# Tokens regrouped by residue modulo 16, and one transposition moved from TensorE to VectorE

## The chip, the cores and the metric

The kernel runs on one core of a Trainium2 chip. A core has five engines that run side by side, each with its own instruction queue that is worked off strictly in order: TensorE (PE in the profile; its weight loads are shown apart as PEld), VectorE (DVE), ScalarE (ACT), GpSimd (POOL) and SyncE (SP). They wait for one another through semaphores. Sixteen DMA engines move data between the core's memory SBUF and HBM; the transfers are issued from the queues of SP, ACT and POOL. Matrix products land in PSUM. The metric is the time of one execution on the device, in microseconds.

## The reference

Two layers over 512 tokens of width 1024. Layer 0 is attention in three groups of 8 heads; in each group a token sees keys at a stride (the dilation) within a window, and the three results are mixed by their log-sum-exp:

```
A_GROUPS = ((128, 1), (512, 4), (2048, 16))      # (window, dilation)
for g, (window, dilation) in enumerate(A_GROUPS):
    # query t attends to t + j*dilation, |j| <= window/(2*dilation)
    o_g, l_g = dilated_window_attention(q[:, :, g], k[:, :, g], v[:, :, g], window, dilation)
w = softmax(stack(lses), axis=2);  o = sum(w[..., None] * outs)
```

With 512 tokens the third group (dilation 16) lets a token see exactly the 32 tokens of its own residue modulo 16. Layer 1 is grouped-query attention over all tokens with a rotary embedding by row and column. Both layers also attend to 256 memory tokens, multiply by a SiLU gate, go through an output projection and are added to the residual: `x = x + y @ w_out`.

## The kernel before

**Tokens.** The 512 tokens stand in four blocks of 128, one token a partition. Block `c` (or `b`) holds the tokens whose residue modulo 4 is `c`: partition `p` holds token `4p + c`. The views that say so are `xv` (L1053, the input, read again at L1003 for the residual sum), `v0w` (L1182, a scratch tensor `v0d` in HBM that takes the values of the first group) and `ov` (L1671, the output); the rotary tables are laid out likewise on the host. So the second group (dilation 4) needs scores within a block only, and so does the third: its scores are the same 128x128 products with a mask that keeps keys of the same residue modulo 4 within the block, which is modulo 16 over all tokens. The first group (dilation 1) needs the tokens in their natural order; `qk0` is written in that order with a stride (L1264, L1265), and its values go through `v0d`.

**Projections.** Each projection is a seven-product scheme (`s_chunk`, L390) with matmuls at L176, L177 and L180. Weights come as 512 KB tiles `wl` on SP's queue (L261), some are summed by POOL's accumulating DMAs (L297, L307) or by DVE (L292), ACT makes a rounded copy `wh` (L323) and DVE the rest `wo` (L333). A ring of four such pairs feeds TensorE.

**The order of the work.** One core, no scheduler: a driver (`Driver`, L48) counts slots, one for each group of projection matmuls, and in between lets generators place the attention work of the head before. The text of every engine's queue follows from the slots alone.

**The start.** Memory tokens first, while `x` is loaded in four transfers (L1071); ACT squares `x` (L527), POOL makes the factor, DVE scales (L534), TensorE transposes (L540). `setup` (L1097) loads the mask and the rotary tables.

**A head of layer 0.** `head_chunk` (L1230) projects, `attn_a` (L1274) attends. Scores `sa` come from L1301 (first group, `o = 0`) and L1305 (second and third, `o = 1`); DVE adds the mask and takes the maximum (L1311), ACT makes exponentials (L1283), statistics go through HBM (`ds`) to change between the two token orders, `scale` (L1372) weights the probabilities, and `turn` (L1381) transposes them on TensorE into PSUM `pt` (L1392) and copies them to SBUF `pT` (L1396 for `o = 1`, `split` for `o = 0`). For `o = 1` there are two parts of four 128x128 blocks: `k = 0` is the second group, copied by ACT, `k = 1` the third, copied by DVE. `pv` (L1407) multiplies by the values, `comb` (L1421) adds the two orders.

**The end.** The last output projection stores eight pieces of 256 KB: four on ACT's queue as they are ready (L1674), the last four on ACT's and SP's (L1682).

Of the kernel before, what the change touches and what calls it, by code (L numbers as in the profile page):

```python
# [131 lines left out]
def trunk_kernel(ctx: ExitStack, tc: tile.TileContext, x, mem, wall, norm_g, mem_norm_g, gcol,  # L132
# [857 lines left out]
    def out_proj(YW, ys, src, evac, tiles, half=False, last=None):  # L990
# [10 lines left out]
        def ev(q, u, t):  # L1001
            b, n = 2 * (int(q[0]) - 1) + u, int(q[1]) - 1
            G.dma_start(t, src[b][:, n * 512:(n + 1) * 512], accum_op=ALU.add)  # L1003
            yield 2
            done.add((n, b))
# [47 lines left out]
    xv = x.rearrange("(p c) d -> c p d", c=4)  # L1053
# [43 lines left out]
    def setup():  # L1097

        nc.sync.dma_start(mask, mask_d)
        nc.sync.dma_start(tabA, tab_a.rearrange("p (b c d) -> p b c d", b=2, c=4))  # L1100
        nc.sync.dma_start(grA[:, 0:3], qn_a[0:1, :, 0:32].to_broadcast([128, 3, 32]))
        nc.sync.dma_start(grA[:, 3:6], kn_a[0:1, :, 0:32].to_broadcast([128, 3, 32]))
        yield 4
        V.tensor_tensor(gk, gc[:, 0:3], gc[:, 3:6], ALU.mult)
        V.tensor_scalar(gk, gk, QS, None, ALU.mult)
        V.tensor_scalar(gc[:, 6:8], gc[:, 6:8], QS, None, ALU.mult)
        V.memset(gk[0:32, :], 1.0)
        V.tensor_scalar(grA[:, 0:3], grA[:, 0:3], QS, None, ALU.mult)
# [121 lines left out]
    def head_chunk(h):  # L1230
# [7 lines left out]
        def ev(q, u, t):  # L1238
# [19 lines left out]
            def put():  # L1258
# [3 lines left out]
                else:  # L1262
                    A.copy(qs[:, :, cs], p[:, 1:3])
                    A.copy(qk0[:, 0].rearrange("p (a c) -> p c a", c=4)[:, b], p[:, 0])  # L1264
                    V.tensor_scalar(qk0[:, 1].rearrange("p (a c) -> p c a", c=4)[:, b], p[:, 3], gk[:, 0:1], None, ALU.mult)  # L1265
# [8 lines left out]
    def attn_a(h, qk0, qs, ks, v12, n_done):  # L1274
# [64 lines left out]
        nc.sync.dma_start(nat_v[:, :, 0, :], stp[:, 0])  # L1339
        nc.sync.dma_start(str_v[:, :, 1, :], stp[:, 1])  # L1340
        yield Y[3]
        nc.sync.dma_start(oth[:, 0], nat_v[:, :, 1, :])
        nc.sync.dma_start(oth[:, 1], str_v[:, :, 0, :])
# [37 lines left out]
        def turn(o):  # L1381

            if o:
                parts = [[(b, k) for b in range(4)] for k in range(2)]
                pts[o] = m4(name="pT").rearrange("p (k t) -> p k t", k=2)
            else:
                parts = [[(0, 0), (3, 1), (0, 1), (1, 0)], [(1, 1), (2, 0), (2, 1), (3, 0)]]
                pts[o] = [m4(F32R, "pT") for _ in range(2)]
            for i, part in enumerate(parts):
# [4 lines left out]
                def copy(pt=pt, i=i):  # L1394
                    if o:
                        (V.tensor_copy if i else A.copy)(pts[o][:, i], pt)  # L1396
# [10 lines left out]
        def pv(o):  # L1407
# [13 lines left out]
            def comb():  # L1421
                if o:
                    A.copy(rs, oo)
                else:
                    V.tensor_tensor(rs.rearrange("p (b a) -> p b a", b=4), oo.rearrange("p (a b) -> p b a", b=4),
                                    rs.rearrange("p (b a) -> p b a", b=4), ALU.add)
# [51 lines left out]
    def setup_b():  # L1478
        tb_raw = s2(name="tbraw").rearrange("p (c b e) -> p c b e", c=2, b=4)
        nc.sync.dma_start(tb_raw, tab_b.rearrange("p (c b e) -> p c b e", c=2, b=4))  # L1480
# [190 lines left out]
    ov = out.rearrange("(p c) d -> c p d", c=4)  # L1671

    def ev_o2(n, b, o):
        nc.scalar.dma_start(ov[b][:, n * 512:(n + 1) * 512], o[n])  # L1674
# [6 lines left out]
    def last_o2(n, b, t, c):  # L1681
        (nc.sync if n else nc.scalar).dma_start(ov[b][:, n * 512 + c.start:n * 512 + c.stop], t[:, c])  # L1682
# [107 lines left out]
```

## Time and profile before

| what | value |
|---|---|
| three runs, median (lowest to highest) | 943.32 us (943.01 to 944.55) |
| the profiled execution, first to last instruction | 940.4 us |
| PE, PEld busy | 932.0 us (99%), 819.4 us (87%) |
| DVE, ACT, POOL busy | 799.6, 691.6, 348.4 us (85%, 74%, 37%) |
| TensorE clock granted | 1.000 |
| DMA traffic | 207.15 MB in 89285 packets |

The page gives no other time for the profiled execution than its span; the median of the runs is 2.9 us above that. Durations in the profile are of single instructions, which overlap on an engine that pipelines them, so a busy time is a union and not a sum. The DMA share is the mean over the sixteen DMA engines, and it can pass 1.

### The profile page before, as it was taken

The numbers are of one execution on the slowest core, as the hardware profiler recorded it, in microseconds if no ns is written. First come the engines' busy times: TensorE is split into PE (matmuls) and PEld (weight loads), VectorE is DVE, ScalarE is ACT, GpSimd is POOL, SyncE is SP. The second block draws the span as 40 slices with busy tenths as digits, with TensorE's granted clock in tenths as the row PEclk, the third lists the DMA queues.
The fourth block names the chain that finished last, engine by engine and source line by source line (L and its number), as shares of the span: only waits on it lengthen the run. The fifth ranks groups of instructions, "written<-read, shape, count | busy, mean of one in ns | idle before, by whom it ended". The sixth has DMA issues, their size and how long they took to land.

```text
span 940.4 us, 16301 instructions
## 1 busy us (share of the span) xinstructions
PE 932.0 (99%) x5500; PEld 819.4 (87%) x5500; DVE 799.6 (85%) x1443; ACT 691.6 (74%) x1720; POOL 348.4 (37%) x494
## 2 busy tenths in 40 slices
PE   8999999999999999999999999999999999999998
PEld 6889888888888888888889998888988999999886
DVE  6998776879888888889788999877998998689978
ACT  7775788677768686867675768537878887789773
POOL 3412425455554545463836111214252440110122
PEclk9999999999999999999999999999999999999999
DMA  9999937869787878696867979979985686785777
GB/s 346 387 259 324 316 93 189 278 133 262 155 251 146 261 155 267 158 268 136 242 177 190 269 202 249 291 239 317 270 201 118 171 240 167 198 225 121 200 159 179
DMA packets 89285, 207.15 MB, mean 220 GB/s; under 512 B 25201, under 2 KB 34417, under 8 KB 89202
## 3 DMA queue, kind: packets, MB, share of 16 engines
q1 hardware_dynamic: 68674, 140.51, 43.5%
q0 software_dynamic: 19520, 63.97, 36.8%
q10 hardware_dynamic: 1008, 1.64, 0.5%
q8 instruction: 43, 0.70, 0.3%
q14 instruction: 40, 0.33, 0.1%
HBM read 158.31 MB, written 11.08 MB: 180 GB/s over the span
## 4 chain that ended last, share of the span: by engine, by line
PE 95%; DVE 2%; ACT 1%; DMA 1%; issue 0%; SPq 0%; DVEq 0%; ACTq 0%
PE pj L177 25%; PE pj L176 25%; PE pj L180 25%; PE qT L645 3%; PE sa L1305 2%; PE oo L1413 2%; PE pt L1392 1%; PE ptb L1619 1%; PE sa L1301 1%; PE xT L540 1%; PE ob L180 1%; PE ob L177 1%; PE ob L176 1%; PE sb L171 1%; PE sb L170 1%; PE sb L172 1%
## 5 line engine op out<-in xcount | busy, mean ns | idle before, releaser
L333 DVE TENSOR_TENSOR wo<-wl,wh 128x1024 fp32r<-128x1024 f32 x258 | 316.3, 1232 | 6.9 <-ACT wh L323 6.7
L323 ACT CAST wh<-wl 128x1024 fp32r<-128x1024 f32 x258 | 272.1, 1061 | 31.0 <-PE pj L177 17.4
L176 PE MATMUL pj<-wh,hS 128*128 128x512 f32 (+1 forms) x416 | 154.4, 380 | 0.0
L177 PE MATMUL pj<-wh,hS 128*128 128x512 f32 (+1 forms) x416 | 149.0, 367 | 0.0
L176 PE MATMUL pj<-wh,h 128*128 128x512 f32 (+1 forms) x312 | 115.3, 378 | 0.0
L177 PE MATMUL pj<-wh,h 128*128 128x512 f32 (+1 forms) x312 | 111.7, 367 | 0.0
L488 POOL TENSOR_TENSOR rstd<-mse,half 128x4 f32<-128x4 f32 (+2 forms) x98 | 103.4, 1056 | 8.2
L180 PE MATMUL pj<-wo,hS 128*128 128x512 f32 (+1 forms) x416 | 99.5, 366 | 0.0
L177 PEld LDWEIGHTS pj<-wh,hS 128*128 128x128 f32 x416 | 78.7, 189 | 11.2
L176 PEld LDWEIGHTS pj<-wh,hS 128*128 128x128 f32 x416 | 78.6, 189 | 11.1 <-DVE sn L420 0.2
L487 POOL TENSOR_SCALAR mse<-hss 128x4 f32<-128x4 f32 (+1 forms) x88 | 47.8, 543 | 101.9 <-ACT junk L633 94.2
L180 PEld LDWEIGHTS pj<-wo,hS 128*128 128x128 f32 x416 | 72.5, 189 | 13.1
L633 ACT ACTIVATE junk<-sn 128x128 f32<-128x128 f32 x264 | 79.4, 311 | 2.7 <-DVE sn L411 2.6
L398 ACT COPY sn<-pj 128x512 f32<-128x512 f32 x122 | 67.1, 588 | 17.8 <-PE pj L180 17.0
L1249 POOL TENSOR_TENSOR ta<-sn,tabs 128x128 f32<-128x128 f32 (+1 forms) x64 | 35.8, 566 | 119.0 <-DVE sn L638 91.8
L180 PE MATMUL pj<-wo,h 128*128 128x512 f32 (+1 forms) x312 | 74.5, 365 | 0.0
L307 POOL DMA_DIRECT2D wl<-wl x34 | 30.2, 897 | 113.3 <-DVE wo L333 73.3
L261 POOL DMA_DIRECT2D wl<-in_wall_dram x40 | 38.0, 966 | 80.4 <-DMA wl<-in_wall_dram 41.0
L177 PEld LDWEIGHTS pj<-wh,h 128*128 128x128 f32 x312 | 59.0, 189 | 8.4
L176 PEld LDWEIGHTS pj<-wh,h 128*128 128x128 f32 x312 | 59.0, 189 | 8.2
L420 DVE TENSOR_TENSOR sn<-pj,sn 128x512 f32<-128x512 f32 x89 | 60.8, 684 | 5.7 <-PE pj L180 5.3
L180 PEld LDWEIGHTS pj<-wo,h 128*128 128x128 f32 x312 | 54.3, 189 | 9.7
(290 smaller groups left out, 2367.2 us busy)
## 6 DMA issues: line engine op xcount, KB each, us to landing
wl<-in_wall_dram SPq DMA_DIRECT2D x224, 512.0 KB, 7.4
wl<-wl POOLq DMA_DIRECT2D x68, 512.0 KB, 5.5
wl<-in_wall_dram POOLq DMA_DIRECT2D x44, 512.0 KB, 8.5
od<-o SPq DMA_DIRECT2D x11, 256.0 KB, 5.4
og<-od SPq DMA_DIRECT2D x10, 256.0 KB, 9.5
x<-in_x_dram SPq DMA_DIRECT2D x4, 512.0 KB, 9.1
v0d<-sn SPq DMA_DIRECT2D x8, 256.0 KB, 8.5
acc<-in_x_dram POOLq DMA_DIRECT2D x8, 256.0 KB, 6.2
```

What stands on the lines that cost most here:

```text
L176: T.matmul(o, a, b, start=start, stop=False, skip_group_check=True)
L177: T.matmul(o, c, d, start=False, stop=False, skip_group_check=True)
L180: T.matmul(o, a, b, start=False, stop=stop, skip_group_check=True)
L261: queue.dma_start(t, wall[d], **how)
L323: A.copy(wh, self.tile[self.items[i]])
L333: V.tensor_tensor(wo, self.tile[key], wh.bitcast(F32), ALU.subtract)
L398: A.copy(t, b)
L420: V.tensor_tensor(t, b, t, ALU.subtract if q == "12" else ALU.add)
L487: G.tensor_scalar(e, ss, EPS, None, ALU.add)
L488: G.tensor_tensor(r, e, half[:, 0:n], ALU.pow)
L633: A.activation(jk, p[:, j * 128:(j + 1) * 128], AF.Square, scale=by, accum_out=ss[:, j:j + 1])
L1249: G.tensor_tensor(ta[:, 0:n], xn[:, 0:n, 0:32], ropeA[:, 0, b, s0:s0 + n], ALU.mult)
```

## The change

Within a block the tokens now stand by their residue modulo 16: partition `p = 32 i + a` of block `c` holds token `16 a + 4 i + c`. The tokens that the third group lets see each other are then 32 neighbouring partitions, and its 128x128 probabilities are zero outside four 32x32 blocks on the diagonal. Such a matrix is transposed by VectorE's 32x32 block transposition: in `turn(1)` the four TensorE transpositions of `k = 1` and DVE's copy out of PSUM give way to one `V.transpose` from SBUF to SBUF. To set the new order the views of `x`, `v0d`, `out`, the tables and the statistics get a further dimension; the second half of the mask is loaded row-permuted into a tile `ok` and column-permuted by two POOL copies; `qk0` and `comb` get one more dimension. The tables on the host are as before.

```
-            G.dma_start(t, src[b][:, n * 512:(n + 1) * 512], accum_op=ALU.add)
+            G.dma_start(t, src[b][..., n * 512:(n + 1) * 512], accum_op=ALU.add)
...
-    xv = x.rearrange("(p c) d -> c p d", c=4)
+    xv = x.rearrange("(a i c) d -> c i a d", i=4, c=4)
...
-        nc.sync.dma_start(mask, mask_d)
-        nc.sync.dma_start(tabA, tab_a.rearrange("p (b c d) -> p b c d", b=2, c=4))
+        nc.sync.dma_start(mask[:, 0:256], mask_d[:, 0:256])
+        ok = s2(name="ok")[:, 0:256]
+        nc.sync.dma_start(ok, mask_d[:, 256:512].rearrange("(a i) k -> i a k", i=4))
+        nc.sync.dma_start(tabA.rearrange("p b c d -> p (b c d)"), tab_a.rearrange("(a i) f -> i a f", i=4))
...
+        for g in range(2):
+            G.tensor_copy(mask[:, 256 + g * 128:384 + g * 128].rearrange("p (i a) -> p i a", i=4), ok[:, g * 128:(g + 1) * 128].rearrange("p (a i) -> p i a", i=4))
...
-    v0w = v0d.rearrange("(p c) d -> c p d", c=4)
+    v0w = v0d.rearrange("(a i c) d -> c i a d", i=4, c=4)
...
-        nc.sync.dma_start(v0w[2 * i + u][:, j * 512:(j + 1) * 512], t)
+        nc.sync.dma_start(v0w[2 * i + u][:, :, j * 512:(j + 1) * 512], t)
...
-                    A.copy(qk0[:, 0].rearrange("p (a c) -> p c a", c=4)[:, b], p[:, 0])
-                    V.tensor_scalar(qk0[:, 1].rearrange("p (a c) -> p c a", c=4)[:, b], p[:, 3], gk[:, 0:1], None, ALU.mult)
+                    q0, k0 = [qk0[:, n].rearrange("p (a i c) -> p c i a", i=4, c=4)[:, b] for n in range(2)]
+                    A.copy(q0, p[:, 0].rearrange("p (i a) -> p i a", i=4))
+                    V.tensor_scalar(k0, p[:, 3].rearrange("p (i a) -> p i a", i=4), gk[:, 0:1], None, ALU.mult)
...
-        ds = dram.tile([S, 2, 2], F32, name="ds")
-        nat_v = ds.rearrange("(b p) o s -> p b o s", b=4)
-        str_v = ds.rearrange("(p b) o s -> p b o s", b=4)
+        ds = dram.tile([2, S, 2], F32, name="ds")
+        nat_v = ds.rearrange("o (b p) s -> o p b s", b=4)
+        str_v = ds.rearrange("o (a i b) s -> o i a (b s)", i=4, b=4)
...
-                parts = [[(b, k) for b in range(4)] for k in range(2)]
+                parts = [[(b, 0) for b in range(4)]]
                 pts[o] = m4(name="pT").rearrange("p (k t) -> p k t", k=2)
+                drv.late(lambda: V.transpose(pts[1][:, 1].rearrange("p (b q) -> p b q", b=4), prob[1][:, :, 128:256]))
...
-                        (V.tensor_copy if i else A.copy)(pts[o][:, i], pt)
+                        A.copy(pts[o][:, 0], pt)
...
-    ov = out.rearrange("(p c) d -> c p d", c=4)
+    ov = out.rearrange("(a i c) d -> c i a d", i=4, c=4)
...
-        nc.scalar.dma_start(ov[b][:, n * 512:(n + 1) * 512], o[n])
+        nc.scalar.dma_start(ov[b][:, :, n * 512:(n + 1) * 512], o[n])
...
-        (nc.sync if n else nc.scalar).dma_start(ov[b][:, n * 512 + c.start:n * 512 + c.stop], t[:, c])
+        (nc.sync if n else nc.scalar).dma_start(ov[b][:, :, n * 512 + c.start:n * 512 + c.stop], t[:, c])
```

No instruction changes its place on an engine. SP's queue, at the start of the program, before and after the change (`x` is the input, `v0d` the scratch in HBM, `wl` weights; the numbers are the extents of what is written):

```order
 L1069 DMA gc<-in_gcol_dram 128x10
-L1071 DMA x<-in_x_dram 128x1024 x2
+L1071 DMA x<-in_x_dram 128x1x1024 x2
 L261 DMA wl<-in_wall_dram 128x1024 x2
-L1071 DMA x<-in_x_dram 128x1024 x2
+L1071 DMA x<-in_x_dram 128x1x1024 x2
 L261 DMA wl<-in_wall_dram 128x1024 x18
-L1186 DMA v0d<-sn 128x512 x2
+L1190 DMA v0d<-sn 4x32x512 x2
```

The same transfers stand in the same places; where HBM is written, the outermost extent goes from 128 to 4. For the loads the side in HBM, which the row does not show, goes from 128 rows to 4 x 32 rows in the same way, as the new view `c i a d` says.

ACT's queue at its end, where the results are stored (`acc` and `sn` are result tiles):

```order
-L398 COPY sn<-pj 128x512 x2
-L1674 DMA out_dram<-acc 128x512 x4
-L1682 DMA out_dram<-sn 128x512 x2
+L398 COPY sn<-pj 128x512 x2
+L1680 DMA out_dram<-acc 4x32x512 x4
+L1688 DMA out_dram<-sn 4x32x512 x2
```

Again the outermost extent alone moves, and on SP's queue the last two stores change alike.

DVE's queue in a head of layer 0 after the change, at `turn(1)` (`p` are probabilities, `qk` the keys of the first group):

```order
L1384 TENSOR_SCALAR p<-p,c 128x256 x2
L1384 TENSOR_SCALAR p<-p,c 128x192
L1270 TENSOR_SCALAR qk_2355<-qT,gk 128x4x32
L1391 STREAM_TRANSPOSE pT<-p 128x512
L1316 ISA p,st<-sa,tabs 128x256
```

Where the block transposition stands, a `COPY pT<-pt 128x512` stood; it no longer waits for TensorE. TensorE's row at that place goes from `MATMUL pt<-ident,p 128x128 x8` to `x4`.

More of the change, by code (lines that the diff above doesn't have):

```diff
@@ L1424, in comb @@
                 else:
-                    V.tensor_tensor(rs.rearrange("p (b a) -> p b a", b=4), oo.rearrange("p (a b) -> p b a", b=4),
-                                    rs.rearrange("p (b a) -> p b a", b=4), ALU.add)
+                    rv = rs.rearrange("p (b i a) -> p b i a", b=4, i=4)
+                    V.tensor_tensor(rv, oo.rearrange("p (a i b) -> p b i a", b=4, i=4), rv, ALU.add)
             drv.late(comb)
```

10 lines of the change are left out of this document (5 added, 5 removed).

## The prediction, made before the changed kernel was run

> **What bounds the kernel now.** I read the page from the top: the busy times, the slices, and the shares of the chain that ended last.
>
> ```profile
> span 940.4 us, 16301 instructions
> PE 932.0 (99%) x5500; PEld 819.4 (87%) x5500; DVE 799.6 (85%) x1443; ACT 691.6 (74%) x1720; POOL 348.4 (37%) x494
> PE   8999999999999999999999999999999999999998
> DMA  9999937869787878696867979979985686785777
> PE 95%; DVE 2%; ACT 1%; DMA 1%; issue 0%; SPq 0%; DVEq 0%; ACTq 0%
> ```
>
> TensorE is the bound in every slice: it idles 8.4 us in all (940.4 - 932.0), nearly all at the two ends. So a matmul taken out of the middle is worth its whole time, and a delay counts where it makes TensorE wait: at the start, where it waits for the first data, and after its last product, where the stores set the end. The DMA row is the other thing to see: the engines are full for the first five slices (117 us) and have room from the sixth on.
>
> **The change part by part. First, what it removes:** per head four of eight transpositions. The timeline of PE in the first head:
>
> ```profile
> 236.54 1.04 PE L1392 MATMUL pt<-ident,p 128*128 128x128 f32 x8
> 237.42 1.06 PE L1305 MATMUL sa<-ks,qs 128*128 128x128 f32 x8
> ```
>
> Eight take 0.88 us from their start to the next start, 0.11 each. Eight heads lose 4 each, 32 x 0.11 = **3.5 us**. The group row below gives 16.6/128 = 0.13, hence 4.2; that holds the tail of the last one, which others overlap, so I take 3.5.
>
> **What it adds on VectorE and ScalarE** (groups of PE, DVE and ACT):
>
> ```profile
> L1392 PE MATMUL pt<-ident,p 128*128 128x128 f32 x128 | 16.6, 273 | 0.0
> L1396 DVE COPY pT<-pt 128x512 f32<-128x512 f32 x8 | 5.5, 691 | 0.0
> L1379 DVE TENSOR_SCALAR p<-p,c 128x256 f32<-128x256 f32 x42 | 12.2, 347 | 0.0
> L1265 DVE TENSOR_SCALAR qk<-qT,gk 128x128 f32<-128x128 f32 x32 | 14.6, 455 | 13.0 <-ACT qk L1264 12.7 <-issue 0.3
> L1261 DVE TENSOR_SCALAR ks<-qT,gk 128x128 f32<-128x128 f32 x32 | 10.4, 348 | 17.8 <-ACT ks L1260 17.7
> L1264 ACT COPY qk<-qT 128x128 f32<-128x128 f32 x32 | 12.8, 401 | 0.0
> 260.00:309.00 49.00, 49.00 (x260) 41.57 (x259) 41.48 (x94) 36.01 (x108) 26.29 (x40) 1.00 0.79 203
> ```
>
> The block transposition of 512 columns replaces a copy of 691 ns. No row shows one: from below 347 ns (an SBUF operation of 256 columns), from above 1.8 us (four strided pieces of 455). I take the copy's 691, the nearest in size. The strided writes of `qk0` (step 16 bytes, now 64) cost 107 ns over L1261's dense ones; a doubling would add 0.1 us to each of the eight writes a head. Together -0.3 to +1.9 us a head, on engines that idle 7.5 us (DVE, 49.00 - 41.48) and 13 us (ACT) in a head's window, the last row. On the path: 0. Without that cover a head would pay 1.2 us, 10 us in all, at the upper price. The copy's wait for TensorE goes away; nothing new waits on DVE.
>
> **What it does to the transfers** is the large part. In HBM the outermost extent of `x`, `v0d`, `out`, half the mask, the tables and `ds` becomes 4 instead of 128. Is a transfer then still spread over sixteen DMA engines? The trace has one transfer whose outermost extent is small, the first of all, one row of 4 KB. The list of DMA issues, then stretches with the DMA share and the GB/s at the end of the row:
>
> ```profile
> x<-in_x_dram SPq DMA_DIRECT2D x4, 512.0 KB, 9.1
> v0d<-sn SPq DMA_DIRECT2D x8, 256.0 KB, 8.5
> out_dram<-acc ACTq DMA_DIRECT2D x4, 256.0 KB, 2.2
> row<-in_mem_norm_g_dram SPq DMA_DIRECT2D x1, 4.0 KB
> ```
> ```profile
> 1.60:1.80 0.20, 0.00 (x0) 0.00 (x0) 0.00 (x0) 0.20 (x1) 0.00 (x0) 1.00 0.05 20
> 18.00:20.00 2.00, 2.00 (x10) 1.63 (x9) 2.00 (x2) 2.00 (x6) 0.00 (x0) 1.00 1.02 408
> 55.00:60.00 5.00, 5.00 (x23) 4.13 (x22) 4.92 (x7) 5.00 (x9) 0.00 (x0) 1.00 1.05 230
> 60.00:70.00 10.00, 10.00 (x46) 8.29 (x45) 9.97 (x14) 6.58 (x10) 1.78 (x2) 1.00 1.03 275
> 90.00:100.00 10.00, 10.00 (x74) 9.47 (x74) 5.55 (x7) 6.24 (x14) 3.05 (x5) 1.00 1.04 347
> 117.00:141.00 24.00, 24.00 (x133) 20.82 (x132) 19.13 (x32) 20.95 (x61) 6.42 (x10) 1.00 0.39 94
> 937.00:938.00 1.00, 0.00 (x0) 0.00 (x0) 0.06 (x1) 0.00 (x0) 0.00 (x0) 1.00 1.02 383
> ```
>
> The row of 4 KB keeps 0.05 x 16 = 0.8 of one engine busy at 20 GB/s, one engine's 1/16 of the 408; and it alone of these issues has no landing time, so its completion was reported otherwise than that of the 128-row transfers. Those fill all sixteen (1.02). So the outer extent seems to set the width, and I take 4 rows of 32 to run on **four engines**, the same four each time. One row of data can only sit on one engine, though, so this is an inference and gets a chance, not a certainty.
>
> [...]
>
> *The start.* One engine moves 408/16 = 25.5 GB/s. A transfer of `x` is 512 KB: 1.3 us on sixteen, 5.1 on four, 3.9 more. Four make the four engines 15.4 us late. When `x` is needed (the answer for the tile `x`, then ACT, DVE and PE in time):
>
> ```profile
> L1071 SPq DMA_DIRECT2D x<-in_x_dram x4: 328/328/328, 9.7 to 15.8; - x4
> DMA to landing us min/median/max: 8.7/9.1/9.3
> ```
> ```profile
> 18.63 0.64 ACT L527 ACTIVATE sq<-x 128x512 f32<-128x512 f32 x1
> 28.79 0.65 ACT L527 ACTIVATE sq<-x 128x512 f32<-128x512 f32 x1
> 33.53 1.40 DVE L534 SCALAR_TENSOR_TENSOR x<-x,rstd,row 128x512 f32<-128x512 f32 x2
> 36.39 1.03 PE L540 MATMUL xT<-ident,x 128*128 128x128 f32 x8
> 72.51 0.21 DVE L1108 TENSOR_SCALAR grA<-grA 128x96 f32<-128x96 f32 x1 [2.29 <-DMA grA<-in_qn_a_dram]
> ```
>
> The last `x` lands at 15.8 + 9.1 = 24.9, with four engines at 40.3. From its first square (28.79) to its transposition (36.39) are 7.6 us, in which it also queues for other work; the pieces alone, two squares of 0.65 and the scaling of 1.40, are 2.7. So TensorE gets it between 43.0 and 47.9: 6.6 to 11.5 us late. I take **8**, near the lower, since the other work will be done by then. ACT stands in this wait with its weight copies queued behind, and those late weights are inside the same delay.
>
> *To 100 us.* Each store of `v0d` (256 KB) costs the four engines 64 instead of 16 KB, 1.9 us more, eight of them 15; `ok` and `tabA` 1 each. The engines have no room there (1.05, 1.03). The first to feel it is DVE, which already waits 2.29 us for `grA`, issued right behind: by then the four engines owe 15.4 + 3.9 + 1.9 = 21 us, less the 8 that TensorE has lost as well, so DVE stands 13 us more. It is full before (9.97 of 10) and gets back 2.3 and 4.5 us of idle time by 100 us, the latter from the fifth row. Weights queue on the same engines, but the 0.39 from 117 us on lets them catch up. Of 0 to 13 us I take **5**. POOL's two mask copies wait for `ok` in front of the accumulating weight transfers; same lateness, not counted twice.
>
> *The end:*
>
> ```profile
> 930.25 3.12 ACTq L1674 DMA_DIRECT2D out_dram<-acc  x4
> 935.14 1.70 ACTq L1682 DMA_DIRECT2D out_dram<-sn  x2
> ```
> ```profile
> 935.73 1.70 SPq L1682 DMA_DIRECT2D out_dram<-sn  x2
> ```
> ```profile
> 938.80:939.00 0.20, 0.00 (x0) 0.00 (x0) 0.00 (x0) 0.00 (x0) 0.00 (x0) 1.00 0.02 0
> ```
>
> Eight stores of 256 KB: 0.7 us each on sixteen engines at 383 GB/s, 2.7 on four. Data flows some 1.5 us after an issue (the 2.2 to landing less 0.7), from 931.8; eight in a row end at 931.8 + 21.9 = 953.7 instead of 938.8: **+14.9 us**. If the first four had drained by 935, only the last four would count: 935.1 + 1.5 + 11 = 947.6, +8.8.
>
> *The rest.* The eight residual sums from `x` (POOL's queue) are issued well ahead; 0, at most 3. The statistics `ds` become fewer and longer pieces, and nothing on the path waits for them; 0.
>
> Sum: 940.4 - 3.5 + 8 + 5 + 14.9 = 964.8 us of span; with the 2.9 us that the median of the runs lies above the profiled span, **968**. From the bounds: 940.4 - 4.2 + 6.6 + 0 + 8.8 + 2.9 = 955 to 940.4 - 3.5 + 11.5 + 13 + 14.9 + 3 + 2.9 = 982.
>
> **The rivals.** *Wide (faster).* The transfers keep sixteen engines: the row count, 128 on both sides, may decide rather than the outer extent, and the bytes and row lengths are unchanged. Then only the 3.5 us are left: **939.8**. For it: all 128-row transfers look alike; against it: the one narrow row. *Narrow but rotating.* Four engines, other ones each time. Then no queue of four builds up: the first `x` is 3.9 us late with 0.2 us of slack (lands at 18.4, taken at 18.63), the later ones have more slack, and at the end the last store alone takes 2.0 us longer: 943.3 - 3.5 + 3.7 + 2.0 = **945.5**. *VectorE becomes the bound (slower).* In one place: the head's window, once the block transposition and the writes at a step of 64 bytes cost DVE more than its 7.5 us of idle time. At 10 us a head it would be 8 x 2.5 - 3.5, **960**; the bounds above stop at 1.9, so this is remote.
>
> **How the numbers follow.** Four fixed engines 0.79, wide 0.13, rotating 0.06, VectorE 0.02. 0.2% of 943.3, 1.9 us, is about what a measurement of this kernel can tell from no change. Faster is the wide case but for a remainder: 0.12; the rotating case lies on the edge of slower, half of it and the remainder are no change: 0.04; slower 0.84. The likeliest case's own range is 955 to 982; to hold eight in ten, and since late weights could be covered better than I think, the low end goes down to 945, which leaves out the wide case and little else: 945 to 982.
>
> **What would show it.** Right: `x`, `v0d` and the results without a landing time in the list of DMA issues, like the one-row transfer; the last stretch between TensorE's end and the end of the span some 20 us long at a DMA share of about 0.25 and 95 GB/s; ACT's square of the third and fourth `x` waiting for DMA, PE idle near 36 us; DVE's wait for `grA` over 10 us; `pt` at 96 instead of 128, and DVE's transposition near 0.7 us with PE still 99% busy from 150 to 590 us. Wrong: 408 GB/s while `x` is loaded and an end some 5 us after the last stores begin to be issued, as now (935.73 to 940.4; then wide); front late but tail as before, or the reverse, if one estimate of the two was off; a DVE row above 5 us for the transposition. The estimate that could be most off is the 5 us up to 100 us.

## The result, and the profile after

| | before | after |
|---|---|---|
| runs, median (lowest to highest) | 943.32 us (942.37 to 944.55), five runs | 1044.89 us (1044.66 to 1045.42), four runs |
| ratio, 95% interval | | 1.1079 (1.1066 to 1.1092) |
| span of the profiled execution | 940.4 us | 1043.2 us |
| mean TensorE clock granted | 1.000 | 0.956 |

Slower by 102 us: as forecast in sign, but some four times as much in size, since 968 was predicted (25 us) and 982 was the high end (39 us). One disturbed execution each of the changed kernel, of `x16_pad` and of `x_groups` (1575, 1555 and 4073 us) is left out throughout; that of `x_groups` was the profiled one, so that of its trace only the transfers of the first 34 us are read here.

The page of the changed kernel: the span, the busy times, two rows of the slices, and the shares of the chain that ended last.

```profile
span 1043.2 us, 16239 instructions
PE 942.6 (90%) x5468; PEld 824.8 (79%) x5468; DVE 798.2 (77%) x1443; ACT 691.6 (66%) x1720; POOL 346.8 (33%) x496
PE   7596969999999999999999999607999999999991
PEclk9699989999999999999999999957999999999996
PE 73%; issue 5%; DVE 5%; DMA 3%; ACT 2%; POOL 1%; DVEq 0%; POOLq 0%; ACTq 0%
```

TensorE, 99% busy before, now has holes in four places: the first two slices, slices 4 and 6, slices 26 to 28, and the end. The last but one is the widest, and it lies where the prediction put 0, at most 3 us. TensorE's busy time rose too, from 932.0 to 942.6, though it has 32 instructions less. The row PEclk shows why: the granted clock is low in slices 2, 6, 27, 28 and 40, in the holes and just behind them.

How late each place is follows from the same matmul in both timelines. Before the change:

```profile
28.01 0.39 PE L177 MATMUL pj<-wh,act 128*128 128x512 f32 x1
104.52 0.39 PE L177 MATMUL pj<-wh,h 128*128 128x512 f32 x1
581.24 0.48 PE L176 MATMUL pj<-wh,yS 128*128 128x512 f32 x1
665.30 0.39 PE L176 MATMUL pj<-wh,hS 128*128 128x256 f32 x1
935.12 0.61 PE L180 MATMUL pj<-wo,ylS 128*128 128x512 f32 x2
```

and after it:

```profile
46.31 0.49 PE L177 MATMUL pj<-wh,act 128*128 128x512 f32 x1
145.63 0.40 PE L177 MATMUL pj<-wh,h 128*128 128x512 f32 x1
618.89 0.48 PE L176 MATMUL pj<-wh,yS 128*128 128x512 f32 x1
750.73 0.39 PE L176 MATMUL pj<-wh,hS 128*128 128x256 f32 x1 [0.75 <-DVE sn L420]
1020.48 0.61 PE L180 MATMUL pj<-wo,ylS 128*128 128x512 f32 x2
```

TensorE is 18.3 us late once `x` is in, 41.1 late at the matmul that stood at 104 us, 37.7 after the eight heads (these won 3.4 back), and 85.4 after the first output product. It is still 85.4 late at its last product. From the end of that (935.7 and 1021.1) to the end of the span it takes 22.1 us instead of 4.7, another 17.4. Together 102.8, the difference of the spans (1043.2 - 940.4).

What TensorE waited for in those holes, and then DVE, after the change (the total, how often, the longest):

```profile
PE pj L176 <- DVE acc L806: 33.3, 2, 30.4
PE pj L180 <- DVE wo L333: 15.3, 2, 8.0
PE xT L540 <- issue: 9.3, 1, 9.3
PE qT L1219 <- DVE sn L638: 8.8, 1, 8.8
PE xT L540 <- DVE x L534: 5.0, 1, 5.0
```
```profile
DVE acc L806 <- DMA acc<-in_x_dram: 52.1, 4, 32.6
DVE sn L638 <- POOL rstd L488: 17.1, 5, 13.0
DVE sq L525 <- DMA x<-in_x_dram: 13.5, 1, 13.5
DVE grA L1112 <- DMA grA<-in_qn_a_dram: 12.0, 1, 12.0
```

The residual sums are transfers that POOL issues (L1003): each adds a piece of `x` to a tile `acc` that holds a product. At L806 DVE adds a further product to that tile and has to wait until `x` is in it; 32.6 us is DVE's longest wait in these lists.

The transfers, in the list of DMA issues after, and four stretches (the DMA share and the GB/s close a row):

```profile
x<-in_x_dram SPq DMA_DIRECT2D x4, 512.0 KB
acc<-in_x_dram POOLq DMA_DIRECT2D x8, 256.0 KB, 10.3
```
```profile
20.00:22.00 2.00, 2.00 (x11) 1.65 (x10) 0.29 (x1) 0.00 (x0) 0.00 (x0) 1.00 0.26 96
34.00:40.00 6.00, 0.00 (x0) 0.00 (x0) 0.00 (x0) 0.00 (x0) 0.00 (x0) 0.69 1.03 223
682.00:692.00 10.00, 0.00 (x0) 0.00 (x0) 0.00 (x0) 0.00 (x0) 1.09 (x1) 0.50 0.22 30
1030.00:1035.00 5.00, 0.00 (x0) 0.00 (x0) 0.00 (x0) 0.00 (x0) 0.00 (x0) 0.50 0.26 102
```

The first and last rows are what four engines look like: a share of 0.26 and some 100 GB/s. (The missing landing times are a weaker sign than the prediction made of them: the weights `wl` on the same queue, unchanged transfers of 128 rows, have lost theirs as well.) The second row wasn't foreseen: all sixteen engines are full, nobody computes, and only 223 GB/s flow, where the same stretch before had 411. In the third one residual sum runs at 30 GB/s and everything waits for it, TensorE at half its clock.

What the change was made for is there:

```profile
L1391 DVE STREAM_TRANSPOSE pT<-p 128x512 f32<-128x512 f32 x8 | 5.5, 693 | 0.0
```

The block transposition takes 693 ns, the copy that it replaced took 691. TensorE has 96 transpositions there where it had 128, and the writes of the keys at four times the step cost no more than before (445 ns, 455 then).

### The profile page after: what moved, and what is told of

It is laid out like the page before. It is cut to its first block, busy times and chain, and to the rows that moved or that the text cites. A ratio compares the mean times of both kernels' runs of the same rounds, so it can differ in the third digit from the quotient of the medians.

```text
span 1043.2 us, 16239 instructions
## 1 busy us (share of the span) xinstructions
PE 942.6 (90%) x5468; PEld 824.8 (79%) x5468; DVE 798.2 (77%) x1443; ACT 691.6 (66%) x1720; POOL 346.8 (33%) x496
## 4 chain that ended last, share of the span: by engine, by line
PE 73%; issue 5%; DVE 5%; DMA 3%; ACT 2%; POOL 1%; DVEq 0%; POOLq 0%; ACTq 0%
PE pj L176 19%; PE pj L177 19%; PE pj L180 18%; PE qT L645 2%; DVE wo L333 2%; DMA wl<-in_wall_dram 2%; PE sa L1310 1%; PE oo L1419 1%; PE ptb L1625 1%; PE sa L1306 1%; PE pt L1398 1%; DMA acc<-in_x_dram 1%; PE ob L180 1%; PE ob L177 1%; PE ob L176 1%
## 5 line engine op out<-in xcount | busy, mean ns | idle before, releaser
L323 ACT CAST wh<-wl 128x1024 fp32r<-128x1024 f32 x258 | 271.7, 1060 | 35.3 <-PE pj L177 14.9
L176 PE MATMUL pj<-wh,h 128*128 128x512 f32 (+1 forms) x312 | 117.1, 383 | 1.8 <-ACT sn L398 1.8
L177 PE MATMUL pj<-wh,h 128*128 128x512 f32 (+1 forms) x312 | 113.1, 371 | 0.0
L487 POOL TENSOR_SCALAR mse<-hss 128x4 f32<-128x4 f32 (+1 forms) x88 | 45.5, 517 | 103.1 <-ACT junk L633 95.4
L261 POOL DMA_DIRECT2D wl<-in_wall_dram x40 | 37.7, 943 | 100.8 <-DMA wl<-in_wall_dram 53.9
L176 PEld LDWEIGHTS pj<-wh,h 128*128 128x128 f32 x312 | 60.3, 193 | 10.6 <-ACT sn L398 2.2
L177 PEld LDWEIGHTS pj<-wh,h 128*128 128x128 f32 x312 | 60.2, 193 | 8.5
## 6 DMA issues: line engine op xcount, KB each, us to landing
acc<-in_x_dram POOLq DMA_DIRECT2D x8, 256.0 KB, 10.3
```

Of the source, the lines that this page charges most:

```text
L176: T.matmul(o, a, b, start=start, stop=False, skip_group_check=True)
L177: T.matmul(o, c, d, start=False, stop=False, skip_group_check=True)
L261: queue.dma_start(t, wall[d], **how)
L323: A.copy(wh, self.tile[self.items[i]])
L487: G.tensor_scalar(e, ss, EPS, None, ALU.add)
```

## The experiments

All times are medians; each ratio is against the kernel before on the same chip, which had medians of 942.65 to 943.12 us there.

| kernel | us | ratio (95%) |
|---|---|---|
| `wide4`: the change, each regrouped transfer as four of 32 rows | 957.63 | 1.0161 (1.0147 to 1.0174) |
| `i16`: the change with residues modulo 64, extent 16 | 945.89 | 1.0038 (1.0020 to 1.0057) |
| `acc_wide`: the change, only the residual sums as four of 32 rows | 999.38 | 1.0598 (1.0584 to 1.0613) |
| `ring4096`: the change, twice the descriptor memory | 1007.49 | 1.0682 (1.0664 to 1.0700) |
| `ring2048`: its control | 1048.50 | 1.1123 (1.1107 to 1.1140) |
| `acc_alone`: before, only the residual sums narrow | 990.53 | 1.0504 (1.0486 to 1.0521) |
| `x_alone`: before, only `x` narrow | 964.68 | 1.0235 (1.0220 to 1.0249) |
| `x16_alone`: before, only `x` in an extent of 16 | 947.65 | 1.0050 (1.0033 to 1.0067) |
| `x16_pad`: the same, rows 260 KB apart | 946.1 to 950.8 | 1.0061 (1.0038 to 1.0085) |
| `x_groups`: before, `x` in its old order as 16 groups of 8 | 948.34 | 1.0057 (1.0040 to 1.0074) |
| `mid_alone`: before, `v0d`, half the mask, first table narrow | 961.95 | 1.0196 (1.0183 to 1.0210) |
| `v0d_alone`: before, only `v0d` narrow | 959.01 | 1.0168 (1.0155 to 1.0181) |
| `tab_alone`: before, only the mask's half and the table narrow | 944.46 | 1.0015 (1.0007 to 1.0024) |
| `out_alone`: before, only `out` narrow | 958.59 | 1.0166 (1.0152 to 1.0180) |
| `perm`: the transposition, no large transfer regrouped | 944.70 | 1.0021 (1.0012 to 1.0030) |
| `perm2`: the same, put back in order out of PSUM | 942.03 | 0.9991 (0.9981 to 1.0000) |
| `perm3`: the same, SP's queue relieved | 939.62 | 0.9971 (0.9960 to 0.9981) |
| `before67`: before, the seventh head's results kept in SBUF | 942.77 | 1.0002 (0.9993 to 1.0011) |

"Narrow" is an outermost extent of 4, as in the change.

### Is it the extent of 4, or the regrouped order?

`wide4`, on the change, for `x`, `ok`, both tables, `v0d`, the residual sums and `out`:

```
+    def wide(q, dst, view, **how):
+        for i in range(4):
+            q.dma_start(dst[32 * i:32 * i + 32], view[i], **how)
...
-        nc.sync.dma_start(xt[c], xv[c])
+        wide(nc.sync, xt[c], xv[c])
```

> The change, with every regrouped transfer (x, the mask's half, both tables, v0d, the residual sums, out) issued as four transfers of 32 rows each, so that the outermost extent is 32 and not 4; the data, the row order and the transposition on VectorE stay (the statistics stay narrow). Theory (the outer extent of 4 leaves four engines, and that is the whole loss): 943.3 less 3.4 for the transpositions, plus 2 to 6 us for issuing (SyncE took about 0.43 us for an issue, twelve more stand before the last x, and six more on each queue at the end): 942 to 946 us, with landing times back in the list and the residual sums several in flight. Rival (the order of the rows in HBM, with steps of 64 KB between neighbours, is slow by itself): above 1000 us, with low GB/s in the load of x though the DMA share is near 1.

`i16`: `i=4` becomes `i=16` in every view of the change.

> The change with residues modulo 64 in place of 16: i=16 and a=8 in all layouts, so that each transfer has an outermost extent of 16 and stays a single transfer. The third group's result is then not the reference's, since its blocks no longer lie on the diagonal; the work and the number of instructions are the same. Theory (the outer extent sets the number of engines): 940 us (938 to 943), no extra issues, the span ending some 5 us after the last stores are issued. Rival (the regrouped order is slow whatever the extent): 1045 us.

957.6 and 945.9 us: of the 102 us, 87 and 99 are gone when a transfer has 32 or 16 rows in front. So the extent is the main cause. But both lie above the theory, `wide4` 12 us and `i16` 3 us over its upper end, and the rival's sign was there in part: the sixteen engines were busy and moved too little while `x` was loaded. From `wide4`, 14 to 18 us, where the kernel before moves 414 GB/s at a share of 1.03:

```profile
14.00:18.00 4.00, 4.00 (x23) 3.20 (x22) 3.40 (x5) 2.46 (x4) 2.09 (x3) 1.00 1.07 258
```

That is followed up below. It accounts for the smaller part of what `wide4` still loses: TensorE is 3.5 us late there once `x` is in, but 12.5 by the matmul that stood at 150 us, and the stretch behind its last product is 5.2 us longer than before. No run takes these two apart; the transfers are four times as many there.

### The largest hole: the residual sums

`acc_wide` does as `wide4` at L1003 alone. `acc_alone` is the kernel before with one view changed, the converse:

```
-            G.dma_start(t, src[b][:, n * 512:(n + 1) * 512], accum_op=ALU.add)
+            G.dma_start(t, (src[b] if last else xn[b])[..., n * 512:(n + 1) * 512], accum_op=ALU.add)
...
+    xn = x.rearrange("(a i c) d -> c i a d", i=4, c=4)
```

> The change with only the eight residual sums of x (the transfers that GpSimd issues) made of four transfers of 32 rows each; everything else stays narrow. Theory (the eight sums, one at a time on four engines, make TensorE wait 47 us in the middle): 1045 - 47 = 998 us (990 to 1004), TensorE's idle time at 630 to 715 us gone, the start and the tail as in the change. Rival (the sums are only where lateness from the first 150 us comes out): 1035 us or more.

> The kernel before with one thing changed: the eight residual sums read x in an outermost extent of 4; the rows stand in another order than the product they are added to, so the output isn't the reference's. Theory (the sums by themselves wait for one another, 11 us each, whatever came before): 943 + 46 = 989 us (984 to 993), each issued when the one before has landed. Rival (a good part of the 46 needed the late start): 960 to 975.

999.4 and 990.5 us: taken out of the change the sums are worth 45.5 us, put alone into the kernel before 47.5. Both theories hold; the term stands by itself, whatever is late ahead of it. What makes it so large is in POOL's timeline. Before the change they wait for DVE's tiles alone, and pairs go out together (the first two and the last two):

```profile
580.75 1.75 POOL L1003 DMA_DIRECT2D acc<-in_x_dram  x2 [2.90 <-DVE acc L420]
...
609.54 1.75 POOL L1003 DMA_DIRECT2D acc<-in_x_dram  x2 [0.41 <-DVE acc L420]
```

After it, the first and the last three:

```profile
618.90 1.17 POOL L1003 DMA_DIRECT2D acc<-in_x_dram  x1 [4.62 <-DVE acc L420]
...
682.28 1.09 POOL L1003 DMA_DIRECT2D acc<-in_x_dram  x1 [12.75 <-issue]
692.01 1.12 POOL L1003 DMA_DIRECT2D acc<-in_x_dram  x1 [8.64 <-issue]
701.65 1.10 POOL L1003 DMA_DIRECT2D acc<-in_x_dram  x1 [8.52 <-issue]
```

The last are 10 us apart, and 10.3 us is the median to landing: one sum at a time. Each of the seven later sums is issued 0.3 to 0.4 us after the one before it has landed. "issue" is a wait with nothing behind it that the profile shows. The author's guess was that POOL finds no room for the next sum: that the memory which the program sets aside for the descriptors of POOL's transfers (the last number in the line below, 2048 bytes a partition; the ring in what follows) is full with one narrow sum. With twice as much, 1005 to 1020 us were expected. `ring4096` doubles that memory; a buffer had to go for it, and `ring2048` gives up the buffer alone:

```
-NBIG, NM4, NS2, SCRATCH = 7, 23, 14, 2048
+NBIG, NM4, NS2, SCRATCH = 7, 23, 13, 4096
```

> The change with the memory for the descriptors of GpSimd's transfers doubled (2048 to 4096 bytes a partition), for which one of the 14 small s2 buffers is given up; all transfers stay narrow. [...] Rival (four engines are that slow with accumulating transfers, whatever the ring): 1045 us, landings 9 to 15 us apart as before, only the issues earlier.

> Control of the kernel with more memory for descriptors: the change with 13 small s2 buffers in place of 14 and the descriptors' memory as it was. Theory (the memory alone made the 37 us): 1045 us (1042 to 1049), sums one at a time. Rival (the missing buffer moved the work so that the sums went better): 1030 or less.

1007.5 and 1048.5 us: the memory alone brings 41 us back. In `ring4096` the issues are no longer a landing apart:

```profile
638.12 1.08 POOL L1003 DMA_DIRECT2D acc<-in_x_dram  x1 [14.94 <-DVE acc L420]
639.86 1.09 POOL L1003 DMA_DIRECT2D acc<-in_x_dram  x1 [0.65 <-DVE acc L420]
647.19 1.11 POOL L1003 DMA_DIRECT2D acc<-in_x_dram  x1 [6.24 <-DVE acc L411]
652.65 2.21 POOL L1003 DMA_DIRECT2D acc<-in_x_dram  x2 [4.35 <-issue]
```
```profile
653.00:658.00 5.00, 5.00 (x28) 4.23 (x27) 4.23 (x8) 1.08 (x2) 1.86 (x2) 1.00 0.61 91
```

Three are issued before the fourth waits, TensorE is busy in that stretch, and the engines carry 0.61 with several sums in flight, where one alone carried 0.22 in the change; in GB/s it is three times one as well (91 and 30). How much of the 0.61 is the sums' own these answers don't show; if it is most of it, sums in flight together use more than four engines (0.61 x 16 = 9.8, an estimate). The main limit of this term was that memory: 41 us came back with twice as much of it and transfers as narrow as before.

### The start: the narrow load, and a slow shape

> The kernel before with one thing changed: the four loads of x have an outermost extent of 4, as in the change. The tokens then stand in another order than the rest expects, so the output isn't the reference's; the work is the same. Theory (the start lost its 18.4 us by x alone): 943 + 18.4 = 961 us (958 to 964). The prediction's own term was 8: 951 us. Rival (at the start other transfers of the change held TensorE up): below 950.

`x_alone` loads `x` through that same narrow `xn` and leaves all else: 964.7 us, 21.8 more, 0.7 over its theory's range. The hole is the same as in the change, with PE's 10.0 and 5.6 us of waiting at L540 (9.3 and 5.0 above). The term is `x` by itself, and the prediction's 8 was too small. TensorE is 17.9 us late once `x` is in and 21.3 at the matmul that stood at 104 us, so `x` alone costs another 3.4 us later on. To see what else is in it, `x` was loaded in an extent of 16, as 16 groups of 8 rows that lie 256 KB apart in HBM; the rest of the kernel is as before and takes the tokens to stand in their old order:

```
-        nc.sync.dma_start(xt[c], xv[c])
+        nc.sync.dma_start(xt[c], xn[c])
...
+    xn = x.rearrange("(a i c) d -> c i a d", i=16, c=4)
```

> [...] Theory (the order of the rows in HBM makes the load slow by itself, beside the number of engines: in the kernel with residues modulo 64 a packet of 4 KB took about 280 ns and not 160 while x was loaded): 220 to 300 GB/s between 14 and 28 us at a DMA share of 1, and 945 us (943.5 to 947). Rival (it was something else of that kernel): 410 GB/s and 943 us.

947.7 us, slower by 4.8 with all sixteen engines, a little over the theory's range: the loss doesn't need the narrow extent. Two explanations were left, the rows' distance in HBM and the shape. `x16_pad` reads the same order from a copy of `x` with an unused row after every 64; `x_groups` keeps the old order and only breaks the run of 128 rows up, with an unused row after every 32 (the view of `x_wide`, the copy, in the one and in the other):

```
+    xn = x_wide[:, 0:64].rearrange("a (i c) d -> c i a d", c=4)
...
+    xn = x_wide[:, 0:32].rearrange("e (j c) d -> c e j d", c=4)
```

> [...] Theory (rows a large power of two apart in HBM are slow to read): some 400 GB/s between 14 and 28 us, a 4 KB packet near 160 ns, and 943 us (942 to 944). Rival (the order itself, or the extent of 16, is slow): 257 to 335 GB/s at a DMA share of 1 and 947.6 us, as without the unused rows.

> The kernel before with x loaded in its old order of rows, into the same partitions, but as 16 groups of 8 rows: the host lays out a second copy of x with one unused row after every 32, so that the groups don't join to a run of 128. The distances in HBM are those of the kernel before (16 KB between the rows of a group), but for 4 KB a group; the output is the reference's. [...] Rival (the regrouped order in HBM is slow): 160 ns, 410 GB/s and 943 us.

Between 22 and 26 us, one fence each for the kernel before, `x16_alone`, `x16_pad` and `x_groups`:

```profile
22.00:26.00 4.00, 3.88 (x22) 3.03 (x22) 3.09 (x7) 4.00 (x10) 2.98 (x6) 1.00 1.03 410
```
```profile
22.00:26.00 4.00, 3.83 (x21) 3.00 (x20) 0.70 (x2) 3.50 (x12) 2.52 (x5) 1.00 1.04 257
```
```profile
22.00:26.00 4.00, 3.89 (x22) 3.07 (x21) 1.43 (x3) 3.76 (x12) 2.70 (x5) 1.00 1.05 268
```
```profile
22.00:26.00 4.00, 4.00 (x4) 2.62 (x3) 0.00 (x0) 0.00 (x0) 0.00 (x0) 1.00 1.04 277
```

The distance is not it: 260 KB apart is about as slow as 256 (268 and 257 GB/s), and the theory of `x16_pad` falls. The shape is: the old order, the same partitions, 16 KB steps, and still 277 GB/s and 948.3 us, where 945.5 to 949 was expected of a slow shape. (From 30 to 34 us the same trace has 400 GB/s.) The rival to the extent, a slow order of the rows, falls with it as far as these loads of `x` show. What in the shape is slow no run shows, and none shows why the changed kernel moves no more than 223 GB/s from 34 to 40 us.

### The middle

`v0d_alone` and `tab_alone` are the change's lines for `v0w` and for `ok`, `tabA` and the two copies, on the kernel before; `mid_alone` has both.

> The kernel before with only the middle of the change's transfers: v0d is stored, and half the mask and the first table are loaded, in an outermost extent of 4, with GpSimd's two copies of the mask; x, the residual sums and out stay as they were. The output isn't the reference's, since v0d and the mask stand in another order. Theory (the second step of the change's lateness, 22.6 us up to 142 us, is made by these alone): 943 + 22.6 = 966 us (962 to 970). The prediction's term of 5: 948. Rival (half of it needed the late x ahead of it, which had filled the same four engines): 950 to 957.

> The kernel before with only the eight stores of v0d in an outermost extent of 4; v0d then holds the rows in another order, so the output isn't the reference's. Theory (the stores fill the four engines while all sixteen are full, 256 KB in 2.6 us each and SyncE's issue held up behind them): two thirds of the kernel with the whole middle, 943 + 8 to 14 = 951 to 957 us. Rival (they have room from the next issue on): 943 to 946.

> The kernel before with only half the mask and the first table loaded in an outermost extent of 4 and GpSimd's two copies of the mask; the mask stands in another order than the scores, so the output isn't the reference's. Theory (128 KB each on four engines, 1.3 us, and GpSimd held in front of the weights' sums until the mask is there): 943 + 2 to 6 = 945 to 949 us. Rival (GpSimd's wait is what makes the weights late, most of the 22.6): 955 or more.

962.0, 959.0 and 944.5 us, that is 18.9, 16.0 and 1.5 more. `v0d` is nearly the whole term, 2 us over its theory's range; the loads of the mask and the table with GpSimd's copies are below theirs, and `mid_alone` lies at the lower edge of its own. In `v0d_alone`, DVE's wait from 60 to 120 us and POOL's queue at its end:

```profile
DVE sn L638 <- POOL rstd L488: 17.7, 2, 14.5
```
```profile
113.37 1.84 POOL L261 DMA_DIRECT2D wl<-in_wall_dram  x2 [16.87 <-DMA wl<-in_wall_dram]
...
115.61 1.05 POOL L488 TENSOR_TENSOR rstd<-mse,half 128x4 f32<-128x4 f32 x1
```

and SP's queue in the kernel before, then in `v0d_alone`, behind the last store:

```profile
82.50 15.53 SPq L261 DMA_DIRECT2D wl<-in_wall_dram  x6
```
```profile
94.14 30.03 SPq L261 DMA_DIRECT2D wl<-in_wall_dram  x9
```

The stores make the weights behind them late; POOL waits 16.9 us for one of them, and has in its queue behind that the factor `rstd` by which DVE scales queries, which TensorE then transposes (10.3 us of waiting). One late weight tile holds up work that needs no weights, because POOL works in order. The same chain stands in the change, with 13.0 us of DVE's waiting and 8.8 of TensorE's (shown above). There the term is 22.8 (41.1 - 18.3), and alone it is 18.9; the 4 us between them are about the 3.4 that `x` alone still costs in that stretch.

### The tail

> The kernel before with one thing changed: the results are stored with an outermost extent of 4; rows of the output are in another order, so it isn't the reference's. Theory (the tail's loss is the stores alone): 943 + 17.4 = 960.5 us (959 to 962). The prediction's own term of 14.9 would be 958. Rival (the tail is late because its sums are): 945 to 950.

958.6 us, 15.7 more. The stores run alone at the narrow rate, from 945 to 950 us in `out_alone`:

```profile
945.00:950.00 5.00, 0.00 (x0) 0.00 (x0) 0.00 (x0) 0.00 (x0) 0.00 (x0) 0.50 0.26 102
```

The loss is the stores alone, as the theory has it; the time is 0.4 us below its range, and the prediction's 14.9 is nearer to this run than the 17.4 read from the change.

Put together, `x` 21.8, middle 18.9, sums 47.5, tail 15.7 and the 3.4 won make 100.5 of the 101.6 us between the medians.

### The transposition without the regrouped transfers

Nothing forces the new order on the large transfers. `perm` leaves `x`, the residual sums and `out` as they were and makes the order where ACT and DVE read the transposed `x` from PSUM. The gated products are put back in order in SBUF ahead of the output product. The mask and the first table are constants, laid out on the host. `v0d` is stored in runs of 128 rows and read in eight transfers a head instead of three, and the first group's keys take an order within 64 that fits this. Two kinds of small transfer keep an outermost extent of 4: these reads (32 KB each) and the statistics `ds` (4 KB). The line on `xT`, and that on `y`:

```
+            p = p.rearrange("p k (a i) -> p k i a", i=4)
...
+                        f = f.rearrange("p (m i a) -> p m a i", m=4, i=4)
```

> The block transposition with no regrouped transfer of any size: x, out, the residual sums and the second layer's table keep the order of the kernel before; the residues are brought together where ACT and DVE read the transposed x out of PSUM, and the gated products are put back in order where they are prepared for the output product. The mask and the first table are laid out in that order on the host, as constants; v0d is stored 128 rows at a time and read back in eight transfers of 64 rows a head with the first group's keys in a fitting order. The output is to be the reference's. Theory (VectorE's transposition itself is worth the 32 x 0.11 us of TensorE, and everything else of the loss is the transfers): 943.3 - 3.4 = 940 us (938 to 943). Rival (reading and writing at a step costs DVE and ACT at the start and before the output product): 945 to 950 us, with TensorE waiting for them there.

944.7 us, 1.8 more than before, between the theory's 943 and the rival's 945. The start costs nothing (TensorE is nowhere over 0.7 us late up to 280 us), the heads win as they should, and then 4.9 us go at the output product, where the rival had put them. DVE's reads of `y`, before and in `perm`:

```profile
L916 DVE TENSOR_TENSOR yS<-yf,yS 128x512 fp32r<-128x512 f32 x4 | 2.6, 687 | 0.0
```
```profile
L930 DVE TENSOR_TENSOR yS<-yf,yS 128x512 fp32r<-128x512 f32 x4 | 4.3, 1106 | 0.0
```

The elements are read 128 bytes apart, out of SBUF. Out of PSUM such a read cost nothing: in `perm2` ACT's copy of a head's result takes 588 ns out of order, and 588 in order before. So `perm2` puts the gates and the results in order there:

```
+            return t.rearrange("p (m a i) -> p m a i", m=4, i=4), b.rearrange("p (m i a) -> p m a i", m=4, i=4)
...
-            A.copy(t, b)
+            A.copy(*rows(t, b))
```

> As the kernel with the order made where PSUM is read, but the way back is moved too: the gates and the heads' results are put in the order of the rows where they are read out of PSUM (there a read at a step cost nothing: 606 ns for 512 columns as against 611 dense), and no longer in SBUF ahead of the output product (there 1106 ns instead of 687, and 1160 instead of 620 on ScalarE). Theory (the loss of that kernel, 4.9 us between 573 and 579 us, was these SBUF reads): 940 us (938.5 to 942), with no shift of TensorE at 575 us. Rival (runs of four elements are slow from PSUM as well, or each gate is then late by it): 943 to 947 us.

942.0 us, ratio 0.9991 (0.9981 to 1.0000): at the upper edge of the theory's range, and 1.0 us is less than can be told from no change here. The shift at 575 us is not gone, against the theory: TensorE, 3.0 us ahead after seven heads, loses 2.0 at the start of the output product. PE's wait there, DVE's from 574 to 582 us, and SP's queue ahead of it:

```profile
PE pj L176 <- DVE acc L426: 2.0, 1, 2.0
```
```profile
DVE sn L882 <- DMA og<-od: 1.7, 1, 1.7
```
```profile
560.67 9.24 SPq L1347 DMA_DIRECT2D v<-v0d  x8
...
570.50 0.38 SPq L877 DMA_DIRECT2D og<-od  x1
```

DVE multiplies the gates by heads' results that come back from HBM (`og`), and SP issued their loads only after eight reads of `v0d`, which held it for 9.2 us. Most of the transposition's gain was lost to transfers once more, to reads that this version itself had added. `perm3` moves the last head's eight to POOL's queue and keeps the seventh head's results in SBUF; `before67` does the latter to the kernel before:

```
-DIRECT, DIRECT_B = (7,), (3, 4, 5, 6, 7)
+DIRECT, DIRECT_B = (6, 7), (3, 4, 5, 6, 7)
...
+                (G if h == 7 else nc.sync).dma_start(v0[n % 2 * 64:n % 2 * 64 + 64, n // 2], v0r[:, m:m + 16, hs])
```

> The second kernel without regrouped transfers, with SyncE's queue relieved ahead of the output product: the eight reads of v0d of the last head are issued by GpSimd, and the results of the seventh head stay in SBUF (as those of the eighth did) and don't go through HBM. The output is to be the reference's. Theory (TensorE's 2.0 us of waiting there were DVE's 1.73 us for the heads' results from HBM, which SyncE issued late behind the eight reads of v0d): no wait of DVE for og at 577 us, TensorE 3 us ahead to the end, 940 us (939 to 941.5), faster than before by more than can be told from no change. Rival (another wait takes its place, DVE having hardly any idle time there): 941.5 to 943.

> Control: the kernel before with only the results of the seventh head kept in SBUF, as in the third kernel without regrouped transfers. Theory (the kernel before has no wait there that this could remove): 943 us (942.3 to 943.5). Rival (keeping them is a gain of its own): 942 or less.

939.6 and 942.8 us: `perm3` is faster than the kernel before by 3.5 us, ratio 0.9971 (0.9960 to 0.9981), and `before67` is not told from it (1.0002, 0.9993 to 1.0011). PE's wait for DVE there is 0.2 us in `perm3`.

So this version beats both kernels, the one before by about what 32 transpositions on TensorE are worth. Of its two edits only the second was tried alone.

## Why the prediction was right or wrong

| step of the prediction | predicted | measured |
|---|---|---|
| 32 transpositions less | -3.5 | -3.4 |
| DVE's block transposition, covered | 691 ns, 0 | 693 ns, 0 |
| `qk0` written at a wider step | up to +0.1 us each, covered | none (445 ns, 455 before) |
| the start | +8 (6.6 to 11.5) | +18.3 |
| up to 100 us | +5 (0 to 13) | +22.8 |
| residual sums | 0, at most 3 | +47.7 |
| the tail | +14.9 (8.8 to 14.9) | +17.4 |

**Right.** The sign and the main inference: an outermost extent of 4 leaves four of sixteen engines on SP's and ACT's queues, a share of 0.26 at 96 to 102 GB/s where 95 were named. That they are four, and the same four each time, no trace of before shows, which has the one row of 4 KB alone; in the change the share stays at 0.26 from 1030 to 1035 us, with the last stores of both queues in flight. The wide rival and the rotating one fall for these queues; VectorE's rival falls, since the transposition costs what the copy did. The signs named for the tail, for ACT's and DVE's wait for `x` and for `grA` (12.0 us) came.

**Wrong: the step "the eight residual sums are issued well ahead; 0, at most 3".** It failed, and it is most of the 77 us that were missing. The sums are issued well ahead only as long as POOL can issue them; the first issue alone was still on time. The trace of before showed them two by two in flight and a landing of 6.2 us, and the prediction priced neither the transfer on four engines nor what happens if the next must wait for it: from the first of the eight issues to the last it took 82.8 us (618.90 to 701.65), where before it took 29 (580.75 to 609.54). `acc_alone` and `ring4096` with its control settle it.

**Mis-sized: the start, 8 taken, 18.3 measured.** The mechanism was right, as `x_alone` shows, but three things were left out. While `x` was on four engines the rest of the time was counted at full rate, and the mixture moved 223 GB/s; one of SP's four issues of `x` took 6.9 us (the row below) and held the weights back; and TensorE, once it had idled, ran at a lower clock (0.50 from 28 to 30 us, behind 5.0 us of waiting). No run separates what each of the three took.

```profile
L1071 SPq DMA_DIRECT2D x<-in_x_dram x4: 539/1502/6944, 9.2 to 16.1; - x4
```

**Mis-sized: up to 100 us, 5 taken, 22.8 measured.** The prediction named this estimate as the one that could be most off. It looked at DVE's wait for `grA` alone and held that late weights would catch up. `v0d_alone` shows the path that it missed: stores, weights, POOL's queue, `rstd`, DVE, TensorE. The lateness of `ok` in front of POOL's copies, which it named, is worth little: 1.5 us in `tab_alone`, though POOL waits 12.7 us for `ok` in the change.

**About right: the tail.** 15.7 alone, 17.4 in the change, 14.9 predicted.

**Not in the sum at all: the clock.** TensorE's busy time rose by 10.6 us where it should have fallen by 3.5: about 14 of the 102.8 us (10.6 + 3.5, an estimate) are matmuls at a clock that was low in the holes and just behind them, 0.956 on the mean. They lie inside the terms of the table.

**Without effect.** The 1.2 us a head that the prediction names for VectorE and ScalarE "without that cover" does not follow from its bounds of -0.3 to +1.9, but no term rests on it. The 2.9 us that it adds between the profiled span and the runs were 1.8 in the changed kernel's profiled execution (1044.99 and 1043.2).

## What to carry to other kernels

A view of HBM that puts a small extent in front isn't a layout detail: with 4 in front the transfers here had four of sixteen DMA engines (a share of 0.26, 96 to 102 GB/s), and `x` in 16 groups of 8 rows was slow on all sixteen (257 to 277 GB/s at 1.04 to 1.05, where a run of 128 rows had 410). Price it for every queue apart, and ask of each in-order queue what stands behind the slower transfer, since here the largest loss was a queue that couldn't issue the next one and the second largest a queue that waited for a weight in front of work that needed none. Where an order is only needed on the chip, make it where PSUM is read, which cost nothing here (684 ns against 683 on DVE), and then look at which queue the substitute has loaded.

## What the runs showed of the hardware that was not expected

- With 2048 bytes a partition for their descriptors, GpSimd's narrow sums went one at a time, each issued 0.3 to 0.4 us after the one before had landed; with 4096 bytes pairs of them were issued back to back (652.65 us, x2), and the time was 1007.5 us, where the control with 2048 took 1048.5.
- While sixteen groups of eight rows are read, 277 GB/s flow, where it is 410 with runs of 128, in the same order and into the same partitions.
- Reads out of PSUM at a step cost ACT and DVE nothing (ACT 588 ns in `perm2` and 588 before, DVE 684 in `perm` against 683); reads of SBUF 128 bytes apart cost DVE 1106 ns instead of 687 for 512 columns.
- In the change's holes TensorE was granted half its clock (0.50 from 682 to 692 us, and 0.50 from 28 to 30 us behind a wait of 5.0 us), and the matmuls that follow pay for it: 0.63 us each at 31 us in the change, 0.39 at full clock.
